# Gated linear attention in fp32: a gate product from three stacked exact parts, and scores from stacked keys

## The chip, the cores and the metric

The kernel runs on one core of one Trainium2 chip. The metric is the device time of one execution in microseconds (us), lower is better; 1022.12 us is the median of three runs before the change.

## What is computed

One decoder layer over 16 meta tokens and 256 real ones (272 positions, width 2048), all in float32. The mixing half of the layer has four heads of gated linear attention beside a pooling part; the MLP with a hidden width of 8192 follows. Cut to what the change touches:

```python
glr = u @ w_in[:, 3072:3088]                     # (272, 16), u = RMSNorm(h)
g_raw = glr @ gate_w2 + gate_b                   # (272, 512): 4 heads x 128
logg = log_sigmoid(g_raw) / 16
# per head and chunk of 64 tokens:
G = cumsum(logg)
q_dec = q * exp(G);  k_inv = k * exp(-G)
scores = where(causal, q_dec @ k_inv.T, 0)       # (64, 64)
o = scores @ v + q_dec @ S_prev                  # S_prev: state of all chunks before
```

The 256 real tokens are handled as two tiles of 128, that is as two pairs of chunks. Inside a tile the scores of the second chunk with keys of the first are also taken as scores, with their own decay, so that only one state per tile is needed.

## The kernel before, in words

Weights come in blocks of 128 x 2048 (1 MB) over the SP queue, always in the same order. To keep float32 accuracy with fast products, every operand is split into a rounded part `hi` (type fp32r, made by a ScalarE copy, L76) and the rest `lo` (VectorE subtraction, L77), and a product is made of three fp32r calls: hi x hi, hi x lo, lo x hi. Some small products are left as plain fp32 calls.

The stages in order: key projection while the input arrives (L238 to L259), the 16-wide gate projection (L303 to L315), four value strips, two query strips (`ws_strip`, L203 to L205), two strips for the output gate (`as_chunk`, L218 to L220), four pooling strips, the output projection, the first group of the MLP, and from about 300 us on seven repeats of a group stage (`group`, `product` L778 to L780, `half`) that holds most of the time. Small steps of the attention ride along in a list, `side`: after each half block of a strip one entry is taken (`run_side`). There `log_gates` (the gate product at L329, its vector work at L330 to L337), `gates` (L346: sums of the log gates by L353 and L363, exponentials, key products at L365 to L371), `states`, `scores` (L449) and `output` stand one after the other.

The order on each engine is not simply that of the program. The framework plans it from priorities, which follow the program's order, and from its own costs for every instruction, and adds the waits; each engine then works its list in order.

The gate projection makes `glrT`: 48 rows, of which 0 to 15 hold the product with the rounded weight columns, 32 to 47 the product with their rest, the others zero. The gate product (L329) multiplies it with `g2`, 48 rows that hold `gate_w2` twice at the same places, in fp32, once for the 16 meta tokens and once for each tile of 128. In `scores` each tile has two fp32 calls: `ki` (128 keys) with 128 queries, and `ke` (64 keys of the first chunk, decayed to its end) with the 64 queries of the second. Two masked copies (L461) and one ScalarE copy (L464) bring them to `sc`:

```python
pe.matmul(ps[:, ts], ki[h][:, ts], qd[h][:, ts], start=True, stop=True)          # L454
pe.matmul(ps[:64, 256 + 64 * t : 320 + 64 * t],                                  # L455
          ke[h][:, 144 + 64 * t : 208 + 64 * t], qd[h][:, t * P + 64 : (t + 1) * P], ...)
```

Of the kernel before, what the change touches and what calls it, by code (L numbers as in the profile page):

```python
# [7 lines left out]
F32 = mybir.dt.float32  # L8
F32R = mybir.dt.float32r
I32 = mybir.dt.int32  # L10
AF = mybir.ActivationFunctionType
ALU = mybir.AluOpType
PSUM = bass.MemoryType.PSUM

P = 128
D = 2048
KD = D // P
S = 256
NT = S // P
META = 16  # L20
L = META + S
H = 4
# [9 lines left out]
C_TRI, C_AFH, C_AFT, C_AFM, C_ID, C_ONE, C_MASK = 0, 128, 192, 320, 336, 464, 592  # L32
# [4 lines left out]
def hybrid_gla_pool_kernel(  # L37
# [15 lines left out]
    act, dve, pe = nc.scalar, nc.vector, nc.tensor  # L53
# [12 lines left out]
    gq = gstack.enter_context(tc.tile_pool(name="gq", bufs=1))  # L66

    def acc():
        return accp.tile([P, 512], F32, tag="acc", name="acc")

    def gp():
        return gpp.tile([P, 512], F32, tag="gp", name="gp")


    def split(raw, hi, lo):
        act.copy(out=hi, in_=raw)  # L76
        dve.tensor_tensor(out=lo, in0=raw, in1=hi.bitcast(F32), op=ALU.subtract)  # L77
# [40 lines left out]
    ps = gp()  # L118
# [6 lines left out]
    u_hi = big.tile([P, KD, L], F32R, tag="u_hi", name="u_hi")  # L125
    u_lo = big.tile([P, KD, L], F32R, tag="u_lo", name="u_lo")
# [13 lines left out]

    early = gq.tile([P, 768], F32, tag="gw0", name="early")
    glr_raw, gb = early[:, 512:], early[:, :512]
    g2 = gq.tile([48, 512], F32, tag="gw1", name="g2")
    gnw = gq.tile([P, DV], F32, name="gnw")


# [80 lines left out]
    for c in range(4):  # L227
# [6 lines left out]
        for o, n in steps:  # L234
            st = load_x(4 * c + o, n)
            for j in range(n):
                xs[o + j] = st[:, j]
            nc.sync.dma_start(  # L238
                out=raw[:, o * 512 : (o + n) * 512], in_=wts[c, :, o * 512 : (o + n) * 512]
            )  # L240
        w = []
        for hf in range(2):
            hi = hip.tile([P, 1024], F32R, tag="hi", name="hi")
            lo = lop.tile([P, 1024], F32R, tag="lo", name="lo")
            for j in (2 * hf, 2 * hf + 1):
                make_u(4 * c + j, xs[j])
                cs = slice((j % 2) * 512, (j % 2 + 1) * 512)
                split(raw[:, j * 512 : (j + 1) * 512], hi[:, cs], lo[:, cs])
            w.append((hi, lo))
        for jj in ((0,), (1,), (2, 3)) if c == 0 else ((0, 1), (2, 3)) if c < 3 else ((0, 1, 2, 3),):  # L250
            for m in range(H):
                for j in jj:
                    k = 4 * c + j
                    hi, lo = w[j // 2]
                    o = kp[m][:, :L]
                    cs = slice((j % 2) * 512 + m * P, (j % 2) * 512 + (m + 1) * P)
# [11 lines left out]
    kT = [gq.tile([P, L], F32, name=f"kT{h}") for h in range(H)]  # L268
# [27 lines left out]
    def ws_next(lo_t=0):  # L296
        nonlocal ci
        a, b = ci, ci + 1
        ci += 2
        return ws_strip([lambda: raw_chunk(a), lambda: raw_chunk(b)], lo_t)  # L300


    gl = gq.tile([P, KD, 48], F32R, tag="vn2", name="gl")  # L303
    glr_v = glr_raw.rearrange("p (k c) -> p k c", c=RANK)
    dve.memset(gl.bitcast(F32), 0.0)
    act.copy(out=gl[:, :, 0:16], in_=glr_v)
    dve.tensor_tensor(
        out=gl[:, :, 32:48], in0=glr_v, in1=gl[:, :, 0:16].bitcast(F32), op=ALU.subtract
    )
    ps = acc()  # L310
    for k in range(KD):
        pe.matmul(ps[:48, :L], gl[:, k, :], u_hi[:, k, :], start=k == 0, stop=False)
        pe.matmul(ps[:48, :L], gl[:, k, :], u_lo[:, k, :], start=False, stop=k == KD - 1)
    glrT = gq.tile([48, L], F32, name="glrT")
    act.copy(out=glrT, in_=ps[:48, :L])  # L315


    lgs = []
# [1 line left out]
    def log_gates():  # L320
        lg, l_hi, l_lo = (mp.tile([P, 3, 512], d, tag="m", name="lg") for d in (F32, F32R, F32R))
        lgs.extend((l_hi, l_lo))
        g = mp.tile([P, 3, 512], F32, tag="m", name="g")
        dve.memset(g[:, 2], 0.0)
        for t in (2, 0, 1):
            n = P if t < 2 else META
            o = META + t * P if t < 2 else 0
            ps = gp()
            pe.matmul(ps[:n], glrT[:, o : o + n], g2, start=True, stop=True)  # L329
            dve.scalar_tensor_tensor(  # L330
                out=g[:n, t], in0=ps[:n], scalar=rstd[:n, t : t + 1], in1=gb[:n], op0=ALU.mult, op1=ALU.add
            )
        act.activation(lg, g, AF.Abs)
        act.activation(lg, lg, AF.Exp, scale=-1.0)
        act.activation(lg, lg, AF.Ln, bias=1.0)
        dve.scalar_tensor_tensor(out=lg, in0=g, scalar=0.0, in1=lg, op0=ALU.min, op1=ALU.subtract)
        split(lg, l_hi, l_lo)  # L337

    eG = [gq.tile([P, S], F32, name=f"eG{h}") for h in range(H)]
    ki = [gq.tile([P, S], F32, name=f"ki{h}") for h in range(H)]  # L340
    ke = [gq.tile([P, L], F32, name=f"ke{h}") for h in range(H)]
    ken = [gq.tile([P, 2 * DK], F32, name=f"ken{h}") for h in range(H)]
    dtot = gq.tile([P, H], F32, name="dtot")

# [1 line left out]
    def gates(h, t):  # L346
        hs = slice(h * DK, (h + 1) * DK)
        ps = gp()
        if t < 2:
            n = 320 if t == 0 else 192  # L350
            r = cr[:, C_TRI : C_TRI + n]
            for i in range(2):
                pe.matmul(ps[:, :n], lgs[i][:, t, hs], r, start=i == 0, stop=i == 1)  # L353
            ts = slice(t * P, (t + 1) * P)
            act.activation(eG[h][:, ts], ps[:, 0:128], AF.Exp)
            act.activation(ki[h][:, ts], ps[:, 0:128], AF.Exp, scale=-1.0)
            act.activation(ke[h][:, 144 + 64 * t : 208 + 64 * t], ps[:, 128:192], AF.Exp)
            if t == 0:
                act.activation(ke[h][:, 16:144], ps[:, 192:320], AF.Exp)
        else:  # L360
            r = cr[:META, C_AFM : C_AFM + META]
            for i in range(2):
                pe.matmul(ps[:, :META], lgs[i][:META, 2, hs], r, start=i == 0, stop=i == 1)  # L363
            act.activation(ke[h][:, :META], ps[:, :META], AF.Exp)
            dve.tensor_tensor(out=ki[h], in0=kT[h][:, META:], in1=ki[h], op=ALU.mult)  # L365
            dve.tensor_tensor(out=ke[h][:, :144], in0=kT[h][:, :144], in1=ke[h][:, :144], op=ALU.mult)
            kv = ke[h][:, 144:].rearrange("p (t c) -> p t c", t=2)
            dve.tensor_tensor(
                out=kv, in0=kT[h][:, META:].rearrange("p (t c) -> p t c", t=2)[:, :, :64], in1=kv, op=ALU.mult
            )  # L370
            dve.tensor_tensor(  # L371
                out=dtot[:, h : h + 1], in0=eG[h][:, 63:64], in1=eG[h][:, 127:128], op=ALU.mult
            )

    def k_natural(h):
# [4 lines left out]
        act.copy(out=ken[h][:META, P : 2 * P], in_=ps[:META, P : 2 * P])  # L380

    side += [log_gates, idle, idle, idle, idle]
    for h in range(H):
        for t in range(2):
            side.append(lambda h=h, t=t: [gates(h, i) for i in ((0,), (1, 2))[t]])
# [29 lines left out]
    qd = [gq.tile([P, S], F32, name=f"qd{h}") for h in range(H)]  # L415
    qi = [gq.tile([P, S], F32, name=f"qi{h}") for h in range(H)]
    st = mp.tile([P, H, 2, DV], F32, tag="m", name="st")
    sc = [gq.tile([P, S], F32, name=f"sc{h}") for h in range(H)]
# [30 lines left out]
    def scores(h):  # L449
        ps = gp()  # L450
        dve.memset(sc[h], 0.0)
        for t in range(2):
            ts = slice(t * P, (t + 1) * P)
            pe.matmul(ps[:, ts], ki[h][:, ts], qd[h][:, ts], start=True, stop=True)  # L454
            pe.matmul(  # L455
                ps[:64, 256 + 64 * t : 320 + 64 * t], ke[h][:, 144 + 64 * t : 208 + 64 * t],
                qd[h][:, t * P + 64 : (t + 1) * P], start=True, stop=True,
            )
        for t in range(2):
            ts = slice(t * P, (t + 1) * P)  # L460
            dve.copy_predicated(  # L461
                out=sc[h][:, ts], mask=cst[:, C_MASK : C_MASK + P].bitcast(I32), data=ps[:, ts]
            )
        act.copy(  # L464
            out=sc[h][:64].rearrange("p (t c) -> p t c", t=2)[:, :, 64:],
            in_=ps[:64, 256:384].rearrange("p (t c) -> p t c", t=2),
        )

    def output(h, t):
        vs = slice(h * DV, (h + 1) * DV)  # L470
# [18 lines left out]
    for i in range(2):  # L489
        p = ws_next(META)  # L490
# [103 lines left out]
    for g in range(4):  # L594
        p = ws_next(META - (2 << g))
# [11 lines left out]
    h = lp.tile([P, NT, D], F32, name="h")  # L607
# [140 lines left out]
    for s in range(2):  # L748
        ps = [acc(), acc()]
# [3 lines left out]
        for t in range(NT):  # L753
            r = zt.tile([P, 512], F32, tag="r", name="r")
# [147 lines left out]
    for s in range(4):  # L902
# [13 lines left out]
        for t, strips in todo:  # L916
            for q in strips:
                parts = 2 if (t, q) == (1, 3) else 1
                w = 512 // parts
                for i in range(parts):  # L920
                    ps = acc()
                    for k in range(8):
                        hi, lo = tail[q][k // 2]
                        cs = slice((k % 2) * 512 + i * w, (k % 2) * 512 + (i + 1) * w)
                        ts = slice(t * P, (t + 1) * P)
# [4 lines left out]
                    if a + w == D:  # L930
# [4 lines left out]
                        out=h[:, t, a : a + w], in0=h[:, t, a : a + w], in1=fw[:, a : a + w], op=ALU.mult  # L935
# [39 lines left out]
def _constants(np):  # L975
    c = np.zeros((P, N_CONST), np.float32)
    i = np.arange(P)
    same = (i[:, None] // 64) == (i[None, :] // 64)
    upto = same & (i[:, None] <= i[None, :])
    c[:, C_ID : C_ID + P] = np.eye(P)  # L980
    c[:, C_TRI : C_TRI + P] = upto / 16.0
    c[:, C_AFH : C_AFH + 64] = (same & (i[:, None] > i[None, :]))[:, :64] / 16.0
    c[:, C_AFT : C_AFT + P] = (i[:, None] > i[None, :]) / 16.0
    c[:, C_ONE : C_ONE + P] = 1.0
    c[:, C_MASK : C_MASK + P] = upto
    j = np.arange(META)
    c[:META, C_AFM : C_AFM + META] = (j[:, None] > j[None, :]) / 16.0
    return c
# [40 lines left out]
```

## Time and profile before

| | |
|---|---|
| median of three runs | 1022.12 us (1021.54 to 1022.52) |
| the profiled execution's own time | 1019.51 us |
| its span, first to last instruction | 1017.7 us |
| TensorE matmul busy | 1001.1 us (98%) |
| TensorE weight loads busy | 843.9 us (83%) |
| VectorE busy | 829.4 us (81%) |
| ScalarE busy | 600.6 us (59%) |
| mean DMA rate | 194 GB/s |

PE is TensorE's matmul, PEld its weight load, DVE VectorE, ACT ScalarE, SP the queue that issues the loads. A line such as `L329 PE MATMUL gp<-g,glrT 48*16 48x512 x6` reads: program line, engine, operation, output tile from its inputs, rows and columns of the weights, shape of the streamed operand, number of records. Matmuls are pipelined, so records overlap and a record's length is not its cost; the step from one start to the next is. Where a record stands as started together with its own weight load, it waited for that load.

### The profile page before, as it was taken

The page shows a single profiled execution, that of the slowest core. Times are in us where ns is not written, and L with a number is a line of the kernel's source. Part 1 is how long each engine was busy: PE and PEld are TensorE (multiplying, and loading weights), DVE is VectorE, ACT ScalarE, POOL GpSimd, SP SyncE. Part 2 cuts the span into 40 slices and gives each one's busy share as a digit, 9 for nine tenths or more (in the row PEclk, how much of TensorE's full clock was granted, in tenths as well). Part 3 has the DMA queues.
Part 4 walks back from the last instruction along what each step waited for, and adds up shares of the span by engine and source line. Part 5 has one row for each costly group of instructions (what it writes and reads, how often), then busy time and mean ns, then how long its engine had stood idle before and what let it go on. Part 6 is the DMA issues. An engine that isn't in the chain of part 4 may idle for free.

```text
span 1017.7 us, 12947 instructions
## 1 busy us (share of the span) xinstructions
PE 1001.1 (98%) x5073; PEld 843.9 (83%) x5073; DVE 829.4 (81%) x924; ACT 600.6 (59%) x770; POOL 0.2 (0%) x4
## 2 busy tenths in 40 slices
PE   8999999999999899999999999999999999999996
PEld 7999978998888787888888888888888888888885
DVE  7455644776567989979989998997997999899784
ACT  7547544354555655666576576567657657656651
POOL 0000000000000000000000000000000000000000
PEclk9999999999999999999999999999999999999998
DMA  9763443446545283672483565367257357534642
GB/s 342 288 238 138 155 156 131 151 146 252 205 168 196 98 344 109 223 287 109 185 295 141 204 215 203 132 256 272 83 207 289 125 207 252 200 140 153 221 152 83
DMA packets 29821, 197.15 MB, mean 194 GB/s; under 512 B 3456, under 2 KB 3968, under 8 KB 6704
## 3 DMA queue, kind: packets, MB, share of 16 engines
q1 hardware_dynamic: 29760, 196.32, 52.8%
q8 instruction: 40, 0.66, 0.3%
q14 instruction: 21, 0.17, 0.0%
HBM read 194.21 MB, written 2.10 MB: 193 GB/s over the span
## 4 chain that ended last, share of the span: by engine, by line
PE 94%; DVE 4%; DMA 1%; issue 1%; ACT 1%; SPq 0%; ACTq 0%; DVEq 0%
PE acc L219 15%; PE acc L220 15%; PE acc L218 15%; PE sa L779 5%; PE sa L780 5%; PE sa L778 5%; PE acc L203 4%; PE acc L204 4%; PE acc L205 4%; PE sd L779 3%; PE sd L780 2%; PE sd L778 2%; PE gp L629 2%; PE acc L927 1%; PE acc L928 1%; PE acc L926 1%
## 5 line engine op out<-in xcount | busy, mean ns | idle before, releaser
L77 DVE TENSOR_TENSOR lo<-raw,hi 128x1024 fp32r<-128x1024 f32 (+1 forms) x300 | 351.9, 1194 | 115.5 <-ACT hi L76 109.4
L76 ACT CAST hi<-raw 128x1024 fp32r<-128x1024 f32 (+1 forms) x300 | 307.8, 1031 | 211.0 <-PE acc L220 98.5
L76 ACT CAST hi<-blk 128x1024 fp32r<-128x1024 f32 x140 | 147.2, 1054 | 114.6 <-PE acc L220 93.5
L77 DVE TENSOR_TENSOR lo<-blk,hi 128x1024 fp32r<-128x1024 f32 x140 | 166.8, 1221 | 14.4 <-ACT hi L76 12.5
L220 PE MATMUL acc<-hi,z_lo 128*128 128x512 f32 x448 | 175.6, 392 | 0.0
L219 PE MATMUL acc<-lo,z_hi 128*128 128x512 f32 x448 | 175.4, 392 | 0.1
L218 PE MATMUL acc<-hi,z_hi 128*128 128x512 f32 x448 | 174.8, 391 | 0.0
L219 PEld LDWEIGHTS acc<-lo,z_hi 128*128 128x128 f32 x448 | 84.1, 188 | 17.3 <-DVE lo L77 0.4
L218 PEld LDWEIGHTS acc<-hi,z_hi 128*128 128x128 f32 x448 | 84.1, 188 | 17.2
L220 PEld LDWEIGHTS acc<-hi,z_lo 128*128 128x128 f32 x448 | 84.2, 188 | 16.9
L784 DVE TENSOR_TENSOR blk<-blk,raw 128x2048 f32<-128x2048 f32 x42 | 96.0, 2287 | 0.2
L203 PE MATMUL acc<-u_hi,hi 128*128 128x272 f32 (+4 forms) x320 | 92.7, 290 | 0.0
L204 PE MATMUL acc<-u_lo,hi 128*128 128x272 f32 (+4 forms) x320 | 91.3, 286 | 0.0
L205 PE MATMUL acc<-u_hi,lo 128*128 128x272 f32 (+4 forms) x320 | 91.2, 285 | 0.0
L780 PE MATMUL sa<-hi,al 128*128 128x512 f32 x224 | 87.3, 390 | 0.0
L779 PE MATMUL sa<-lo,ah 128*128 128x512 f32 x224 | 87.2, 390 | 0.0
L778 PE MATMUL sa<-hi,ah 128*128 128x512 f32 x224 | 87.2, 389 | 0.0
L203 PEld LDWEIGHTS acc<-u_hi,hi 128*128 128x128 f32 x320 | 60.3, 189 | 1.0 <-issue 0.8
L204 PEld LDWEIGHTS acc<-u_lo,hi 128*128 128x128 f32 x320 | 60.2, 188 | 0.1
L205 PEld LDWEIGHTS acc<-u_hi,lo 128*128 128x128 f32 x320 | 60.1, 188 | 0.0
L621 DVE TENSOR_TENSOR h<-acc,h 128x512 f32<-128x512 f32 (+1 forms) x71 | 46.4, 681 | 4.5 <-PE acc L928 3.6
L779 PEld LDWEIGHTS sa<-lo,ah 128*128 128x128 f32 x224 | 42.0, 188 | 8.8
(236 smaller groups left out, 1549.7 us busy)
## 6 DMA issues: line engine op xcount, KB each, us to landing
raw<-in_wts SPq DMA_DIRECT2D x147, 1024.0 KB, 4.8
blk<-in_wts SPq DMA_DIRECT2D x28, 1024.0 KB, 4.8
xn<-in_x SPq DMA_DIRECT2D x2, 1024.0 KB, 11.3
h<-in_x SPq DMA_DIRECT2D x2, 1024.0 KB, 7.1
out<-h SPq DMA_DIRECT2D x8, 256.0 KB, 2.8
xTs<-in_xT SPq DMA_DIRECT2D x3, 546.0 KB, 9.6
pw<-in_pool_w SPq DMA_DIRECT2D x4, 256.0 KB, 6.0
fw<-in_rows SPq DMA_DIRECT2D x1, 1024.0 KB, 4.4
```

Of the source, the lines that this page charges most:

```text
L76: act.copy(out=hi, in_=raw)
L77: dve.tensor_tensor(out=lo, in0=raw, in1=hi.bitcast(F32), op=ALU.subtract)
L203: pe.matmul(o, hi[:, cs], u_hi[:, k, lo_t:L], start=k == 0, stop=False)
L204: pe.matmul(o, hi[:, cs], u_lo[:, k, lo_t:L], start=False, stop=False)
L205: pe.matmul(o, lo[:, cs], u_hi[:, k, lo_t:L], start=False, stop=k == KD - 1)
L218: pe.matmul(ps[t], a_hi[:, k, ts], hi[:, cs], start=st, stop=False)
L219: pe.matmul(ps[t], a_hi[:, k, ts], lo[:, cs], start=False, stop=False)
L220: pe.matmul(ps[t], a_lo[:, k, ts], hi[:, cs], start=False, stop=sp)
L778: pe.matmul(ps, a_hi[:, k], hi[:, cs], start=start and k == 0, stop=False, **kw)
L779: pe.matmul(ps, a_hi[:, k], lo[:, cs], start=False, stop=False, **kw)
L780: pe.matmul(ps, a_lo[:, k], hi[:, cs], start=False, stop=k == 7, **kw)
L784: dve.tensor_tensor(out=dst, in0=dst, in1=src, op=ALU.add)
```

## The change

The gate projection's weights become 96 columns, three times rounded part and rest side by side (16 + 16). `glrT` becomes fp32r: rows 0 to 63 are rounded on the copy, rows 64 to 95 get what the rounding left. The gate weights come in as six copies of `gate_w2` (96 x 512) and are rounded into `g2r`; rows 32 to 63 hold the rest of the rounding. The gate product is then one fp32r call per tile, with rounded x rounded, rounded x rest and rest x rounded summed in its contraction rows.

For the scores, three key blocks of 64 stand side by side per tile in `kk`: the first chunk's keys, the same keys decayed to the chunk's end, the second chunk's keys. Queries of the first chunk are multiplied with blocks 0 and 1 (128 keys), those of the second with blocks 1 and 2; the mask becomes the causal one of 128 x 128, and the ScalarE copy of the cross block goes.

```diff
-    g2 = gq.tile([48, 512], F32, tag="gw1", name="g2")
+    g2 = gq.tile([96, 512], F32, tag="gw1", name="g2")
+    g2r = gq.tile([96, 512], F32R, name="g2r")
...
-    gl = gq.tile([P, KD, 48], F32R, tag="vn2", name="gl")
+    gl = gq.tile([P, KD, 96], F32R, tag="vn2", name="gl")
     glr_v = glr_raw.rearrange("p (k c) -> p k c", c=RANK)
-    dve.memset(gl.bitcast(F32), 0.0)
-    act.copy(out=gl[:, :, 0:16], in_=glr_v)
-    dve.tensor_tensor(
-        out=gl[:, :, 32:48], in0=glr_v, in1=gl[:, :, 0:16].bitcast(F32), op=ALU.subtract
-    )
+    for r in range(0, 96, 32):
+        act.copy(out=gl[:, :, r : r + 16], in_=glr_v)
+        dve.tensor_tensor(
+            out=gl[:, :, r + 16 : r + 32], in0=glr_v, in1=gl[:, :, r : r + 16].bitcast(F32), op=ALU.subtract
+        )
+    act.copy(out=g2r, in_=g2)
+    dve.tensor_tensor(out=g2r[32:64], in0=g2[32:64], in1=g2r[32:64].bitcast(F32), op=ALU.subtract)
     ps = acc()
     for k in range(KD):
-        pe.matmul(ps[:48, :L], gl[:, k, :], u_hi[:, k, :], start=k == 0, stop=False)
-        pe.matmul(ps[:48, :L], gl[:, k, :], u_lo[:, k, :], start=False, stop=k == KD - 1)
-    glrT = gq.tile([48, L], F32, name="glrT")
-    act.copy(out=glrT, in_=ps[:48, :L])
+        pe.matmul(ps[:96, :L], gl[:, k, :], u_hi[:, k, :], start=k == 0, stop=False)
+        pe.matmul(ps[:96, :L], gl[:, k, :], u_lo[:, k, :], start=False, stop=k == KD - 1)
+    glrT = gq.tile([96, L], F32R, name="glrT")
+    act.copy(out=glrT, in_=ps[:96, :L])
+    dve.tensor_tensor(out=glrT[64:96], in0=ps[64:96, :L], in1=glrT[64:96].bitcast(F32), op=ALU.subtract)
...
-            pe.matmul(ps[:n], glrT[:, o : o + n], g2, start=True, stop=True)
+            pe.matmul(ps[:n], glrT[:, o : o + n], g2r, start=True, stop=True)
...
-    ki = [gq.tile([P, S], F32, name=f"ki{h}") for h in range(H)]
-    ke = [gq.tile([P, L], F32, name=f"ke{h}") for h in range(H)]
+
+    kk = [gq.tile([P, 2, 3, 64], F32, name=f"kk{h}") for h in range(H)]
+    ke = [gq.tile([P, 144], F32, name=f"ke{h}") for h in range(H)]
...
-            act.activation(ki[h][:, ts], ps[:, 0:128], AF.Exp, scale=-1.0)
-            act.activation(ke[h][:, 144 + 64 * t : 208 + 64 * t], ps[:, 128:192], AF.Exp)
+            act.activation(
+                kk[h][:, t, 0::2], ps[:, 0:128].rearrange("p (c b) -> p c b", c=2), AF.Exp, scale=-1.0
+            )
+            act.activation(kk[h][:, t, 1], ps[:, 128:192], AF.Exp)
...
-            dve.tensor_tensor(out=ki[h], in0=kT[h][:, META:], in1=ki[h], op=ALU.mult)
-            dve.tensor_tensor(out=ke[h][:, :144], in0=kT[h][:, :144], in1=ke[h][:, :144], op=ALU.mult)
-            kv = ke[h][:, 144:].rearrange("p (t c) -> p t c", t=2)
-            dve.tensor_tensor(
-                out=kv, in0=kT[h][:, META:].rearrange("p (t c) -> p t c", t=2)[:, :, :64], in1=kv, op=ALU.mult
-            )
+            kv = kT[h][:, META:].rearrange("p (t c b) -> p t c b", t=2, c=2)
+            dve.tensor_tensor(out=ke[h], in0=kT[h][:, :144], in1=ke[h], op=ALU.mult)
+            for c, k0 in ((0, 0), (1, 0), (2, 1)):
+                dve.tensor_tensor(out=kk[h][:, :, c], in0=kv[:, :, k0], in1=kk[h][:, :, c], op=ALU.mult)
...
+        kf = kk[h].rearrange("p t c b -> p t (c b)")
         for t in range(2):
-            ts = slice(t * P, (t + 1) * P)
-            pe.matmul(ps[:, ts], ki[h][:, ts], qd[h][:, ts], start=True, stop=True)
-            pe.matmul(
-                ps[:64, 256 + 64 * t : 320 + 64 * t], ke[h][:, 144 + 64 * t : 208 + 64 * t],
-                qd[h][:, t * P + 64 : (t + 1) * P], start=True, stop=True,
-            )
+            for c in range(2):
+                cs = slice(t * P + c * 64, t * P + (c + 1) * 64)
+                pe.matmul(ps[:, cs], kf[:, t, 64 * c : 64 * c + P], qd[h][:, cs], start=True, stop=True)
...
-        act.copy(
-            out=sc[h][:64].rearrange("p (t c) -> p t c", t=2)[:, :, 64:],
-            in_=ps[:64, 256:384].rearrange("p (t c) -> p t c", t=2),
-        )
...
-    c[:, C_MASK : C_MASK + P] = upto
+    c[:, C_MASK : C_MASK + P] = i[:, None] <= i[None, :]
...
-    g2 = np.zeros((48, 512), np.float32)
-    g2[0:16] = f["gate_w2"][0]
-    g2[32:48] = f["gate_w2"][0]
+    g2 = np.tile(f["gate_w2"][0], (6, 1))
```

## Rows read from the trace of the kernel before

**Rows 1.** The page's part 4, shares of the chain that ended last.
```profile
PE 94%; DVE 4%; DMA 1%; issue 1%; ACT 1%; SPq 0%; ACTq 0%; DVEq 0%
```
**Rows 2.** Timeline of TensorE, 74.9 to 78.6: start, length, line, shapes, records.
```profile
75.28 2.94 PE L329 MATMUL gp<-g,glrT 48*16 48x512 f32 x6
...
78.39 0.29 PE L204 MATMUL acc<-u_lo,hi 128*128 128x272 f32 x1
```
**Rows 3.** Timeline of the weight loads, same stretch.
```profile
76.77 0.19 PEld L329 LDWEIGHTS gp<-g,glrT 48*128 48x128 f32 x1 [0.24 <-issue]
77.20 0.19 PEld L329 LDWEIGHTS gp<-g,glrT 48*128 48x128 f32 x1 [0.24 <-issue]
```
**Rows 4.** One program line, L353: records, shortest, median and longest in ns.
```profile
L353 PE MATMUL gp<-cr,lg x16: 251/291/391, 93.7 to 116.9; 128*128 128x320 f32 x8, 128*128 128x192 f32 x8
```
**Rows 5.** Timeline of TensorE at the end of the gate projection.
```profile
35.76 0.29 PE L313 MATMUL acc<-u_lo,gl 128*48 128x272 f32 x1
35.88 0.29 PE L203 MATMUL acc<-u_hi,hi 128*128 128x272 f32 x1
```
**Rows 6.** Timeline of VectorE, 75 to 90; in brackets the idle time before, and its end.
```profile
76.35 0.74 DVE L330 SCALAR_TENSOR_TENSOR g<-gp,rstd,early 16x512 f32<-16x512 f32 x1 [1.04 <-PE gp L329]
77.40 1.61 DVE L330 SCALAR_TENSOR_TENSOR g<-gp,rstd,early 128x512 f32<-128x512 f32 x2 [0.31 <-PE gp L329]
...
87.95 1.22 DVE L77 TENSOR_TENSOR lo<-raw,hi 128x1024 fp32r<-128x1024 f32 x1
```
**Rows 7.** Timeline of ScalarE at 79.
```profile
79.04 1.49 ACT L333 ACTIVATE lg<-g 128x1536 f32<-128x1536 f32 x1 [2.88 <-DVE g L330]
```
**Rows 8.** Timeline of the weight loads at 90.3.
```profile
90.30 0.19 PEld L205 LDWEIGHTS acc<-u_hi,lo 128*128 128x128 f32 x1
```
**Rows 9.** Timeline of ScalarE, 22 to 28.
```profile
23.17 0.40 ACT L306 CAST gl<-early 128x256 fp32r<-128x256 f32 x1
27.53 0.39 ACT L273 COPY kT<-acc 128x272 f32<-128x272 f32 x1 [3.95 <-PE acc L259]
```
**Rows 10.** Timeline of VectorE, 23 to 30.
```profile
24.13 0.42 DVE L307 TENSOR_TENSOR gl<-early,gl 128x256 fp32r<-128x256 f32 x1
29.04 0.44 DVE L271 COPY kT<-acc 128x272 f32<-128x272 f32 x1 [4.50 <-PE acc L259]
```
**Rows 11.** DMA issues of the first 60 us: KB each, us from issue to landing.
```profile
g<-in_gate_w SPq DMA_DIRECT2D x1, 96.0 KB, 10.2
```
**Rows 12.** Windows: busy us (records) of PE, PEld, DVE, ACT, POOL; clock, DMA share, GB/s.
```profile
14.00:32.00 18.00, 18.00 (x146) 17.99 (x145) 12.12 (x23) 12.28 (x26) 0.00 (x0) 1.00 1.02 403
...
79.00:117.00 38.00, 38.00 (x312) 37.37 (x310) 22.43 (x38) 26.38 (x54) 0.00 (x0) 1.00 0.40 143
```
**Rows 13.** Timeline of TensorE at the first head's scores.
```profile
136.34 0.39 PE L454 MATMUL gp<-qd,ki 128*128 128x128 f32 x2
136.66 0.33 PE L455 MATMUL gp<-qd,ke 128*64 128x64 f32 x2
...
137.93 0.40 PE L219 MATMUL acc<-lo,u_hi 128*128 128x512 f32 x1
138.16 0.40 PE L220 MATMUL acc<-hi,u_lo 128*128 128x512 f32 x1
```
**Rows 14.** Timeline of the weight loads at the first head's scores.
```profile
136.12 0.42 PEld L454 LDWEIGHTS gp<-qd,ki 128*128 128x128 f32 x2
```
**Rows 15.** Timeline of TensorE at 48.4: an fp32 call of 128 x 128.
```profile
48.42 0.38 PE L187 MATMUL gp<-dg,cst 128*128 128x128 f32 x2
```
**Rows 16.** One program line, L368, in ns.
```profile
L368 DVE TENSOR_TENSOR ke<-kT,ke x4: 284/286/289, 99.9 to 119.1; 128x128 f32<-128x128 f32 x4
```
**Rows 17.** Timeline of VectorE, 1 to 4.
```profile
2.24 1.09 DVE L451 MEMSET sc<- 128x256 f32 x4
```
**Rows 18.** Waits of TensorE from 70 us on: total us, times, longest.
```profile
PE acc L219 <- DVE lo L77: 2.6, 1, 2.6
PE sd L779 <- DVE lo L77: 2.1, 1, 2.1
```

## Prediction

> **What bounds the kernel now.** I read the chain that ended last first: 94% of it is TensorE work [rows 1]. So a microsecond taken from TensorE counts, if TensorE does not stop for another engine later. Next I read the two places that the change touches, in the timelines of TensorE and of its weight loads, then what the neighbouring engines have to spare there.
>
> **The gate product, before.** Three fp32 calls, 48 rows deep, show as six matmul records [rows 2]: an fp32 call runs as two passes. One pass of 512 columns takes 0.43 us (weight load at 76.77 to weight load at 77.20, [rows 3]), a call 0.86. An fp32r call is one pass: the gate sums make two fp32r calls for each of four heads and two tiles, and have 16 records [rows 4]. 512 fp32r columns take 0.23 us, L219 to L220 [rows 13]. There are also pauses where the form of the array changes. The pass after 77.20 starts at 77.63 and ends at 78.06; but L203 streams only at 78.26, one step of 0.13 before the L204 of 78.39 [rows 2]. That is 0.20 us: about 0.1 until the weight load is let in, and 0.1 for the load, which is not hidden then. There are three such changes: into 48 rows by 16 columns (a short load, about 0.1), from there to 128 columns, and out.
>
> **The gate product, after.** Three fp32r calls of one pass: 3 x (0.86 - 0.23) = 1.9 us saved with all pauses kept, 2.4 if 96 rows cause none. No row shows a 96-row product. The nearest form shows no pause: after the last product of 128 rows by 48 columns L203 follows in 0.12 us [rows 5]. But a 16-column product stays among the three, and so I keep the two pauses around it: 2.1 us. The Trainium skill ("TensorEngine Tiling (Array Packing)", Key Properties) says that changing the tiling mode drains TensorE, and lists modes of 32, 64 and 128 rows. By it 96 rows are no mode of their own, and the gain would lie nearer 2.4.
>
> **What the earlier gates run into.** The vector work behind the product does not get shorter: three L330 steps, 0.74 for the first and 1.61 for the other two, end at 79.01 [rows 6], and ScalarE's Abs starts at 79.04 [rows 7]. In the new kernel the first result is there 0.43 + 0.2 earlier (one pass of 0.23 for two of 0.43), so L330 starts at 76.35 - 0.63 = 75.7 and, VectorE now being the longer part, ends at 75.7 + 0.74 + 1.61 = 78.05. This chain thus moves 1.0 us, not 2.1. Through ScalarE's queue it carries a split that TensorE needs for the first query strip: its low part is done at 87.95 + 1.22 = 89.17 [rows 6], and the load of its first use is at 90.30 [rows 8], 1.1 us to spare. With TensorE 2.1 and the chain 1.0 earlier nothing is left to spare; so 2.1 is about the cap. I book 2.0.
>
> **Ahead of the gate product** the high and low rows are made. gl takes three ScalarE copies and three subtractions, in place of one each and a memset, at 0.40 [rows 9] and 0.42 [rows 10]. The copy of the 96 x 512 weights and the subtraction on 32 of its rows have twice gl's 256 columns: at most 0.8 each. That is 1.6 us more on either engine, and both idle there: ScalarE 3.95 us behind L306 [rows 9], VectorE 4.50 behind L307 [rows 10]. I book nothing; without that cover the glr product would wait for gl. That product's weights grow from 48 to 96 columns; its step of 0.12 to 0.13 is that of L203 with 128 columns beside it [rows 5]: nothing. glrT's third part is one more subtraction of 0.4 on VectorE; nobody needs glrT before 75 us. The load of the gate weights doubles from 96 to 192 KB. It lands 10.2 us after its issue [rows 11]; at the 403 GB/s of that stretch [rows 12] 96 KB more put off what is queued behind it on SP by 0.24 us. Its reader is needed at 75 and, waiting in ScalarE's queue, has those 3.95 us; of the blocks behind it the first goes to products at 35.9 [rows 5], where ScalarE's split of it already began behind L273 at 27.5 [rows 9]. Nothing.
>
> **The scores, before.** One head takes from the first stream of L454 at 136.34 to the point where fp32r products run undisturbed again (L219 at 137.93 less one step of 0.23): 1.36 us [rows 13]. In it are four fp32 calls, eight passes, and at every call the form changes between 128 and 64 columns. Two passes of L454 from 136.34, 0.11 each, would be streamed by 136.57; L455 is let in only at 136.66 [rows 13]: the same pause as above.
>
> **The scores, after.** Again four calls and eight passes, all with 128 x 128 weights and 64 streamed columns: the form does not change. What is a pass worth that loads 128 columns and streams 64? No row has one. Two passes of L187, with 128 loaded and 128 streamed, start 0.11 apart (two records of 0.27 within 0.38, [rows 15]); so a load of 128 columns or a stream of 128 is 0.11, a stream of 64 is 0.05. Upper end: load and stream one behind the other, 0.16. Lower end: the load hidden altogether, 0.05. I take 0.11, the load as the longer part with the stream beside it: the second load of L454 starts at 136.35 (two of 0.19 within 0.42 from 136.12, [rows 14]), when its first pass starts to stream. So 8 x 0.11 = 0.88, saved 0.48 a head, four heads 1.9 us. The ends: 8 x 0.16 = 1.28 saves 0.3 in all, 8 x 0.05 = 0.4 saves 3.8.
>
> The removed ScalarE copy of the cross block is off the path, and the masked copies stay two a head. In the gates the key products become four VectorE multiplications a head in place of three, one more of 0.29 less what the halved one saves [rows 16]: at most 1.2 us over four heads, on an engine that works 22.4 of the 38 us there [rows 12]. Nothing booked; if it were not covered, the splits behind them would come later by that 0.29.
>
> **Sum.** -2.0 - 1.9 = -3.9 us. The profiled execution took 1019.51 us, its span 1017.7; it becomes 1015.6. The runs' median, 1022.12, is 2.6 above the profiled one; the same saving gives **1018.2**.
>
> **The rivals.** (a) *Given back by the order of the instructions.* The order on each engine is not the program's: sc's memset of line 451 runs at 2.24 us [rows 17]. A planner sets it, and shorter products can turn VectorE's and ScalarE's order later, where TensorE already stops twice for VectorE's low parts, 2.6 and 2.1 us [rows 18]. If one such stop doubles, about 2.4 of the 3.9 are gone: 1020.6. Against it: both stops lie behind VectorE work that TensorE's own results start, so all of it should move along. Chance 0.15.
>
> (b) *Loads do not overlap streams in the scores.* They save 0.3, the sum is -2.3: 1019.8. Against it are the loads of [rows 14]. Chance 0.05. The Trainium skill states such a rule ("TensorE: Matmul & The Clock Gate", The mechanism, in Part 3): a weight load overlaps matmuls in flight only in another row group. The trace disagrees, since the load at 136.35 uses all 128 rows beside a stream that does.
>
> (c) *The log-gate chain becomes the bound.* If the planner puts one more 1.0 us ahead of that split on ScalarE, the gate saves 1.0 only: 1019.2. For it: the spare time is used up. Against it: the planner sees the same chain. Chance 0.07.
>
> (d) *Slower.* From 300 us on, seven group stages repeat. If the new order makes the low part late in each as it is in the first (2.1 us, [rows 18]), six more stops cost 12.6: +8.7, 1030.8. It decides once 5.9 us are lost, with three groups of the six. That no later group shows such a stop now speaks against it. Chance 0.04.
>
> (e) *It does not do what it says.* If a 96-row fp32r product took two passes, the scores alone would be left, -1.9: 1020.2. The records of [rows 4] speak against it. Chance 0.02.
>
> The forecast has the other 0.67.
>
> **How the numbers follow.** About 0.2% (2.0 us) is what a measurement of this kernel can tell from no change. Faster by more than that: the forecast, (b), (c) and a small part of (a), 0.81. Within it: most of (a), and (e), 0.14. Slower: (d) and a little for what I do not see, 0.05. The range: below, no pauses and half of the way to the lower end of a pass, -2.4 - 2.9 = -5.3, and 0.5 for the scatter of the runs: 1016.3. Above, it takes in (a), (b), (c) and (e): 1020.8.
>
> **What would show it.** Right: three gate records instead of six, 0.23 us apart or with a pause, and L203 streaming at about 76.2 instead of 78.26; score passes 0.11 apart without pauses, fp32r products back 0.9 us after the first; everything past 165 us earlier by 3.9, and the stops of [rows 18] as long as now. Wrong: six gate records; passes 0.16 apart; TensorE waiting near 88 us for a low part; new stops behind VectorE after 300 us.

## The result, and the profile after

The changed kernel's runs have a median of 1015.7 us (1015.07 to 1018.02), those of the kernel before beside them 1021.83; the ratio is 0.9946, 95% interval 0.9935 to 0.9958. Two repetitions on other occasions gave 0.995 (0.9938 to 0.9962) and 0.9956 (0.9944 to 0.9969). So it is faster, by some 0.5% where 0.38% was forecast. The median lies 0.6 us below the stated range; by the ratio on the median of the prediction it is 1016.6, inside. The profiled execution took 1015.81 us with a span of 1014.0: 3.7 us less than the one before.

Where the 3.7 us come from is read by laying the two TensorE timelines side by side, the same product in each:

| product | before | after | difference |
|---|---|---|---|
| last of the gate projection | 35.76 | 36.32 | +0.56 |
| first of the gate sums | 93.75 | 91.82 | -1.93 |
| first of the states | 132.42 | 130.49 | -1.93 |
| first of the head outputs | 165.01 | 161.25 | -3.76 |
| first of the second norm (L674) | 332.09 | 328.36 | -3.73 |
| last of the kernel | 1008.78 | 1005.10 | -3.68 |

The gate stretch gave 2.49 us, the scores 1.83, and the start took back 0.56. Nothing is added or lost behind 165 us.

The timeline of TensorE around the gate product after the change (start, length, line, tiles, columns, shape, records; it answers to [rows 2]):

```profile
75.41 0.38 PE L409 MATMUL gp<-cst,vT 128*16 128x128 f32 x2
75.55 0.37 PE L206 MATMUL acc<-u_hi,lo 128*128 128x272 f32 x1
75.76 0.39 PE L334 MATMUL gp<-g2r,glrT 96*16 96x512 f32 x1
75.98 0.29 PE L204 MATMUL acc<-u_hi,hi 128*128 128x272 f32 x1
76.11 0.45 PE L334 MATMUL gp<-g2r,glrT 96*128 96x512 f32 x1
76.40 0.29 PE L205 MATMUL acc<-u_lo,hi 128*128 128x272 f32 x1
76.53 0.41 PE L334 MATMUL gp<-g2r,glrT 96*128 96x512 f32 x1
76.77 0.29 PE L206 MATMUL acc<-u_hi,lo 128*128 128x272 f32 x1
```

Three records, each 0.22 to 0.29 us before the next start, with strip products put between them by the planner, which the prediction did not foresee. No pause of 0.2 is left.

The first head's scores, TensorE and then the weight loads (they answer to [rows 13, 14]):

```profile
134.42 1.00 PE L462 MATMUL gp<-qd,kk 128*128 128x64 f32 x8
135.23 0.48 PE L219 MATMUL acc<-hi,u_hi 128*128 128x512 f32 x1
135.55 0.39 PE L220 MATMUL acc<-lo,u_hi 128*128 128x512 f32 x1
```

```profile
134.19 1.09 PEld L462 LDWEIGHTS gp<-qd,kk 128*128 128x128 f32 x8
```

Eight passes; from 134.42 to L220 less one step of 0.23, 135.32, are 0.90 us, where 0.88 was forecast and 1.36 stood before. The loads, of 0.19 each, start (1.09 - 0.19) / 7 = 0.13 apart on average with the first one early, 0.11 among the others.

The start is the one part of the difference that the change did not make. ScalarE's split of the third piece of weights (the second half of the first block) waits longer for its load, here in the kernel before and then in the one after:

```profile
9.10 1.14 ACT L76 CAST hi<-raw 128x512 fp32r<-128x512 f32 x2 [0.91 <-DMA raw<-in_wts]
```

```profile
9.64 1.14 ACT L76 CAST hi<-raw 128x512 fp32r<-128x512 f32 x2 [1.51 <-DMA raw<-in_wts]
```

The enlarged gate weights are issued only at 13.54 us, when this delay of 0.54 us is already there. In the other nine profiles with the changed gate the end of the gate projection stands between 0.5 us earlier and 1.2 later than before, in the two with the old gate 0.2 and 0.4 earlier; each time all but 0.3 us of the shift is there at this split. It is scatter of the first loads.

TensorE's waits after the change, from 70 us on (they answer to [rows 18]):

```profile
PE acc L220 <- DVE lo L77: 2.6, 1, 2.6
PE sd L779 <- DVE lo L77: 2.1, 1, 2.1
```

The two stops are as long as they were.

### The profile page after: what moved, and what is told of

It is laid out like the page before. It is cut to its first block, busy times and chain, and to the rows that moved or that the text cites. A ratio compares the mean times of both kernels' runs of the same rounds, so it can differ in the third digit from the quotient of the medians.

```text
span 1014.0 us, 12942 instructions
## 1 busy us (share of the span) xinstructions
PE 996.7 (98%) x5070; PEld 843.2 (83%) x5070; DVE 830.3 (82%) x931; ACT 600.0 (59%) x769; POOL 0.2 (0%) x4
## 4 chain that ended last, share of the span: by engine, by line
PE 94%; DVE 4%; DMA 1%; ACT 1%; issue 1%; SPq 0%; ACTq 0%
PE acc L220 15%; PE acc L221 15%; PE acc L219 15%; PE sa L779 5%; PE sa L780 5%; PE sa L778 5%; PE acc L204 4%; PE acc L205 4%; PE acc L206 4%; PE sd L779 3%; PE sd L780 3%; PE sd L778 3%; PE gp L629 2%; PE acc L927 1%; PE acc L928 1%; PE acc L926 1%
## 5 line engine op out<-in xcount | busy, mean ns | idle before, releaser
L220 PE MATMUL acc<-lo,z_hi 128*128 128x512 f32 x448 | 175.4, 392 | 0.0
L220 PEld LDWEIGHTS acc<-lo,z_hi 128*128 128x128 f32 x448 | 84.1, 188 | 17.3 <-DVE lo L77 0.3
```

The costliest lines, as they stand in the source:

```text
L220: pe.matmul(ps[t], a_hi[:, k, ts], lo[:, cs], start=False, stop=False)
```

## The experiments

Theory A: the gain is what TensorE is spared at the two places, 4.3 us, and the rest of the measured difference is scatter. Theory B: the change gives something besides.

**The kernel again, and its two halves.** The first of these is the changed kernel unaltered; the other two take one part of its diff each.

> The changed kernel as it is, beside its two halves. Theory A (the gain is the work taken from TensorE at the two places, and all of it reaches the end): 2.5 us from the gate product and 1.85 from the scores, 4.3 in all, 0.9958 of before; the 5.5 us of the first comparison is then partly scatter between runs. Theory B (something besides, at the start or in a later order, gives about 1.5 us more): 0.9946 again.

```diff
 # gate part only: g2, g2r, gl, glrT and the host's g2 as changed
-            pe.matmul(ps[:n], glrT[:, o : o + n], g2, start=True, stop=True)
+            pe.matmul(ps[:n], glrT[:, o : o + n], g2r, start=True, stop=True)
```

> The gate part alone, scores as before. Theory A: the stretch around the gate product is 2.5 us shorter, everything behind it moves along, 0.9976 of before. Theory B: over 3.5 us, the surplus lies in the gate part (its loads, its gl and g2r steps, or the order). If ScalarE's chain behind the gates were the bound, as the prediction priced it, 2.0 us.

```diff
 # scores part only: kk, ke, the causal mask, scores() as changed
-            pe.matmul(ps[:, ts], ki[h][:, ts], qd[h][:, ts], start=True, stop=True)
+                pe.matmul(ps[:, cs], kf[:, t, 64 * c : 64 * c + P], qd[h][:, cs], start=True, stop=True)
```

> The scores part alone, gate product as before. Theory A: each head's scores 0.46 us shorter, 1.85 us in all, 0.9982 of before. Theory B: over 3 us, the surplus lies here.

Ratios: 0.995 for the whole, 0.9962 (0.995 to 0.9975) for the gate part, 0.9982 (0.9974 to 0.9991) for the scores. The ratios alone do not decide: that of the whole allows both theories, and that of the gate part, 3.9 us, lies on the side of theory B, with 0.9976 just outside its interval. The traces do. In them the gate part alone moves the gate sums by -2.48 us against its start, the scores alone each head by -0.46, 1.85 in all. So the halves add up to the 4.3 us, and neither holds a surplus. But the profile of the gate part ends 0.3 us later than that of before: it loses its gain at two places. TensorE's clock shows where (windows: busy us and records of PE, PEld, DVE, ACT, POOL, then the granted clock, DMA share, GB/s). First the gate part alone behind its two stops, then the changed kernel's first profile around its own two stops:

```profile
353.30:356.60 3.30, 3.30 (x9) 2.56 (x8) 3.30 (x4) 0.11 (x1) 0.00 (x0) 0.50 0.94 318
387.40:390.70 3.30, 3.30 (x9) 2.52 (x9) 3.30 (x4) 1.69 (x2) 0.00 (x0) 0.50 0.00 0
```

```profile
348.00:352.00 4.00, 1.42 (x8) 1.03 (x7) 4.00 (x5) 2.49 (x4) 0.00 (x0) 1.00 0.00 0
381.80:385.20 3.40, 1.30 (x6) 0.74 (x5) 3.40 (x3) 1.96 (x2) 0.00 (x0) 1.00 0.00 0
```

The same kernel can show either. Behind the first stop, the changed kernel in its first profile and in its second:

```profile
351.30:354.60 3.30, 3.30 (x15) 2.69 (x16) 3.30 (x5) 0.71 (x1) 0.00 (x0) 1.00 0.71 233
```

```profile
351.30:354.60 3.30, 3.09 (x7) 2.48 (x8) 3.30 (x5) 0.00 (x0) 0.00 (x0) 0.50 0.63 184
```

Behind each of the two stops, in some executions and not in others, the clock stands at 1.2 GHz instead of 2.4 for a stretch, and in the gate part's profile the products there come 1.6 and 1.4 us later. Of the 13 profiles of this study three show no such stretch, four one behind the first stop (in one of them that stop had moved), three one behind the second, three both. From 8 us to the last products none shows one anywhere else. The lists of runs tell the same by their mean clock. At 0.997 the kernel before has 5 runs of 33, median 1019.74; the changed one 7 of 16, median 1015.6: 4.1 us. At 0.994 before has 10, median 1022.67, the changed one 3, median 1018.02: 4.65. At equal clock, then, the difference is near the 4.3 us of theory A. The gate part alone gives 2.7 us that way (two runs at 0.997, median 1017.0). The 5.5 of the first medians fits more low-clock runs on the side of before: five of the changed kernel's six runs there stand at 0.997 (the six of before have no clock on record). Why there are more is open; with so few runs it may be chance.

**The third repetition.**

> The changed kernel a third time, same chip. Theory A (4.3 us from the two places, the rest of the measured difference is scatter from the clock behind the two stops and from the arrival of the first loads): ratio 0.9946 to 0.997, and at equal clock (0.997 with 0.997) 4.3 us less than before within 0.7.

0.9956 (0.9944 to 0.9969). Its one run at 0.997 took 1015.78 us, 4.0 less than the 1019.74 of before. Its profile ends the gate projection 0.8 us late and shows one stretch at half clock behind the first stop.

**What the pauses are worth in the scores.** This kernel and the two that follow (32 queries, 48 rows) ran once each, so only their traces are read. The old calls in another order:

```diff
             pe.matmul(ps[:, ts], ki[h][:, ts], qd[h][:, ts], start=True, stop=True)
+        for t in range(2):
             pe.matmul(
                 ps[:64, 256 + 64 * t : 320 + 64 * t], ke[h][:, 144 + 64 * t : 208 + 64 * t],
...
```

> The kernel before, with the score calls of a head in another order: both L454 first, then both L455, so that the form of the array changes twice a head and not four times. Theory A (the pauses at changes of form are a large part of what the change saves): a head's block goes from 1.36 to about 1.0 us, 1.4 us over four heads, though the same eight passes run. Rival (the saving comes from streaming fewer columns): 1.36 as before.

Its TensorE timeline at the first head:

```profile
135.85 0.61 PE L454 MATMUL gp<-qd,ki 128*128 128x128 f32 x4
136.39 0.45 PE L456 MATMUL gp<-qd,ke 128*64 128x64 f32 x4
136.77 0.50 PE L218 MATMUL acc<-hi,u_hi 128*128 128x512 f32 x1
137.10 0.39 PE L219 MATMUL acc<-lo,u_hi 128*128 128x512 f32 x1
```

From 135.85 to 137.10 - 0.23 are 1.02 us, 0.34 less than before. Of the 0.46 that the change saves a head, three quarters can be had by the order of the calls alone.

**What sets a pass.** Half of the streamed queries:

```diff
+                cs = slice(cs.start, cs.start + 32)
                 pe.matmul(ps[:, cs], kf[:, t, 64 * c : 64 * c + P], qd[h][:, cs], start=True, stop=True)
...
```

> The changed kernel with 32 streamed queries per score call instead of 64; half of the scores are left out. Theory A (a pass is as long as its load of 128 columns): still 0.11 us a pass, a head's block 0.9 us. Rival (stream and load in part behind each other): 0.03 us less a pass, block 0.65 to 0.7.

The second head of that kernel:

```profile
141.04 0.98 PE L463 MATMUL gp<-qd,kk 128*128 128x32 f32 x8
141.86 0.47 PE L219 MATMUL acc<-hi,u_hi 128*128 128x512 f32 x1
142.17 0.40 PE L220 MATMUL acc<-lo,u_hi 128*128 128x512 f32 x1
```

141.04 to 141.94: 0.90 us, as with 64 queries. A fixed price of a pass, whatever it loads, would show the same; the kernel with reordered calls speaks against it. Its loads of 64 columns:

```profile
136.39 0.31 PEld L456 LDWEIGHTS gp<-qd,ke 128*64 128x64 f32 x4
```

One of them takes 0.14 us, so four within 0.31 start 0.06 apart: half the columns, half the step. So the load of 128 columns sets the pass, 0.11 us, and the stream is hidden beside it.

**What 96 rows are worth.** The gate product over 48 of them:

```diff
-            pe.matmul(ps[:n], glrT[:, o : o + n], g2r, start=True, stop=True)
+            pe.matmul(ps[:n], glrT[:48, o : o + n], g2r[:48], start=True, stop=True)
```

> The changed kernel with the gate product over the first 48 of its 96 rows; the other rows' terms are left out. Theory A (48 rows are another form of the array than 128, 96 rows are not): pauses with open weight loads of about 0.2 us come back at each change, 0.4 to 1.2 us in all by how many products of other lines stand between. Rival (the pauses belonged to fp32): no difference beyond 0.05 us.

```profile
75.40 0.40 PE L334 MATMUL gp<-g2r,glrT 48*16 48x512 f32 x1
75.73 0.39 PE L204 MATMUL acc<-u_hi,hi 128*128 128x272 f32 x1
76.06 0.49 PE L334 MATMUL gp<-g2r,glrT 48*128 48x512 f32 x1
76.48 0.39 PE L205 MATMUL acc<-u_lo,hi 128*128 128x272 f32 x1
```

From one line's start to the next it now takes 0.33 to 0.42 us, where it was 0.13 to 0.29 with 96 rows; the gate stretch gains 1.49 us in place of 2.48. So in this order, with strip products between the calls and thus six changes, one of the 2.5 us comes from the depth and not from fp32r. Back to back, as the calls stood before, there would be three changes and less to gain from the depth; that was not run.

**The same for the other shallow products.** On top of the change, the products with 16 rows get 128, the added ones zeros. The transposes that feed the states become 128 columns wide too, and two ScalarE copies behind them become one:

```diff
-                pe.matmul(ps[:, :META], lgs[i][:META, 2, hs], r, start=i == 0, stop=i == 1)
+                pe.matmul(ps[:, :META], lgs[i][:, 2, hs], r, start=i == 0, stop=i == 1)
...
-    pe.matmul(ps[:, :DV], ken[h][:META, P : 2 * P], vn[2][:, vs], start=True, stop=True)
+    pe.matmul(ps[:, :DV], ken[h][:, P : 2 * P], vn[2][:, vs], start=True, stop=True)
```

> The changed kernel, and the other products with 16 rows made 128 rows deep by zeros (the sums of the meta tokens' gates, the first states, the spread of the meta tokens' norm). Theory A, by which a change in the array's rows costs a pause and an open weight load and the depth itself nothing: four times 0.3 us at the gate sums, four times 0.4 at the states, 0.3 at the norm, 3.1 us less than the changed kernel. Rival (the steps behind 16-row products are slow for another reason, such as waits for their inputs): no difference beyond 0.5 us.

> The kernel with all products 128 rows deep, again, to stand beside the spread one on the same chip. Both theories: 0.992 of before, the stops of 2.6 and 2.1 as they were; half clock behind one or both in part of the runs.

0.9918 (0.9905 to 0.9932) and 0.9939 (0.9925 to 0.9953), the second above the 0.992 expected for it. Beside the changed kernel's runs of the same occasions the medians are 3.2 and 2.5 us lower, where 3.1 was expected. In both traces TensorE at 260 us, counted from the end of the gate projection, is 2.8 us ahead of the changed kernel. First the changed kernel at the first head's states, then this one:

```profile
130.49 0.69 PE L446 MATMUL gp<-vn,ken 16*128 16x256 f32 x2
131.12 0.70 PE L449 MATMUL gp<-vn,ken 128*128 128x256 f32 x2
...
131.88 0.39 PE L220 MATMUL acc<-lo,u_hi 128*128 128x512 f32 x1
```

```profile
129.10 0.59 PE L446 MATMUL gp<-vn,ken 128*128 128x256 f32 x2
129.53 0.59 PE L449 MATMUL gp<-vn,ken 128*128 128x256 f32 x2
...
130.20 0.39 PE L220 MATMUL acc<-lo,u_hi 128*128 128x512 f32 x1
```

From the first stream to L220: 1.39 us with 16 rows, 1.10 with 128. A wait ahead of the first, about 0.1, is gone as well.

**The stops.** Two attempts at the one at 352 us, both on the kernel with full rows. The first moves four VectorE steps away:

```diff
-        dve.tensor_tensor(out=blk(*dst), in0=blk(*x0), in1=blk(*x1), op=op)
+        nc.gpsimd.tensor_tensor(out=blk(*dst), in0=blk(*x0), in1=blk(*x1), op=op)
```

> The kernel with all products 128 rows deep, and the four additions and subtractions of L705 on GpSimd instead of VectorE. Theory A (TensorE's stop at 352 us is VectorE's overload by the operands' preparation, and the stop lets the clock fall in some runs): VectorE has 4.9 us less between 347 and 365, the stop of 2.6 shrinks below 1, 1.5 to 2.5 us less than with the additions on VectorE, and no half clock at 352 in any profile; the stop at 386 stays. Rival (GpSimd's slower steps hold up the operands): the stop moves behind GpSimd and the time does not fall.

The rival held: 0.9957 (0.9943 to 0.9972), worse than without. GpSimd's timeline, then TensorE's waits:

```profile
340.88 13.44 POOL L705 TENSOR_TENSOR a<-a 128x1024 f32<-128x1024 f32 x4 [340.44 <-DVE al L696]
```

```profile
PE gp L629 <- DVE q L757: 4.3, 1, 4.3
PE sd L779 <- DVE lo L77: 2.1, 1, 2.1
PE acc L220 <- DVE lo L77: 0.6, 1, 0.6
```

A step of 1.22 us on VectorE takes 3.4 on GpSimd, and VectorE's own steps beside it (L696) take 2.4 and 2.8 in place of 1.2. ScalarE waits 4.2 us for the first GpSimd result, and VectorE behind it; the old stop shrinks to 0.6, and a longer one stands before L629. Behind that one the clock falls again in this profile, at 351 us, so what theory A says of the clock was not tested. The second attempt changes only how many steps one half block takes:

```diff
-            lambda: operand(2, 0, 1), s5, s7, s6, s3,
+            lambda: operand(2, 0, 1), *s5, *s7, s6, s3,   # s5 and s7 as lists of single steps
```

> The kernel with all products 128 rows deep, and the preparation of operands 5 and 7 split into single steps, so that one half block takes one of them and not two or three. The same work. Theory A (the stop at 352 us is a crowd of preparation steps in front of a low part, and the clock falls only in executions where TensorE has stopped): the stop of 2.6 shrinks below 1, 2 to 3 us less than with the crowd; profiles show no half clock near 352, and the runs scatter less. Rival (VectorE is behind by its whole work there, not by its order): the stop moves to a later half and the time is the same within 0.5 us.

0.9899 (0.9884 to 0.9914), median 1010.12 beside 1013.83 of the crowded one and 1020.9 of before: 3.7 us less than with the crowd, more than the 2 to 3 expected. Its waits of TensorE:

```profile
PE sd L780 <- DVE lo L77: 2.1, 1, 2.1
PE sd L779 <- ACT x L789: 0.2, 1, 0.2
```

The stop of 2.6 is gone, and the trace gains 3.0 us at that place; the rest of the 3.7 fits a clock that falls less often. Its four runs have clocks of 0.995 to 0.997, those of the crowded one 0.994 and 0.995; its profile has no half clock. That the runs scatter less is not shown: they lie 2.5 us apart, the crowded ones 3.2. This is the fastest version of the study.

## Why the prediction was right, and where it was not

**The chain.** Right: TensorE bounds the kernel, and what it was spared reached the end. The traces differ by -3.76 us at 165 and by -3.68 at the end.

**The scores.** Right in mechanism and size: 0.90 us a head for a forecast of 0.88, 1.85 in all for 1.9. That the load sets the pass is shown by the kernel with 32 queries and the shorter loads of the one with reordered calls, that form changes were the greater part by the latter. Rival (b), loads not beside streams, falls with both. The rule that the Trainium skill gives ("TensorE: Matmul & The Clock Gate", The mechanism), overlap only in another row group, does not describe this trace: these loads use all 128 rows beside streams that do. The same section also names a load into a background weight buffer; the prediction left that case out.

**The gate product.** Mis-sized, 2.5 us for a booked 2.0, by two steps. First, "I keep the two pauses around it": with 96 rows none was left, even with 16 columns. The Trainium skill's rule on modes ("TensorEngine Tiling (Array Packing)", Key Properties) pointed the right way, and the kernel with 48 rows, at 1.0 us less gain, agrees with it for rows. Second, the cap "nothing is left to spare" rested on a wrong pairing: the low part done at 89.17 [rows 6] is not the one whose first use is loaded at 90.30 [rows 8]. In the changed kernel the same first use is at 88.55, where VectorE has done only the first of these two:

```profile
86.37 2.35 DVE L77 TENSOR_TENSOR lo<-raw,hi 128x1024 fp32r<-128x1024 f32 x2
```

```profile
88.55 0.19 PEld L206 LDWEIGHTS acc<-u_hi,lo 128*128 128x128 f32 x1
```

The two are done at about 87.6 and 88.7. Which one the load reads is found by counting: it opens the seventeenth half block of the strips, and the first of the two is the seventeenth split of such a half block. In the kernel before the seventeenth is this one:

```profile
81.72 1.23 DVE L77 TENSOR_TENSOR lo<-raw,hi 128x1024 fp32r<-128x1024 f32 x1 [2.71 <-ACT hi L76]
```

It was done seven us ahead of its use, so there was no cap at 2.1. The chain did move less than TensorE, as forecast: ScalarE's Abs starts at 78.27 where it was 79.04 [rows 7], 1.3 us earlier against the late start.

**The covers** held: gl's six steps, g2r and the doubled load end before 26.6, and TensorE has no gap at the gate projection.

**The order of the instructions** (rivals (a) and (c)) did change: the split that ran at 80.64 runs at 84.92. It cost nothing here, but it took most of what was to spare: of the seven us one is left in the changed kernel. No new stop appeared (rival (d)), and each call is one pass (rival (e) fell).

**The run-to-run part** was missing. I set 0.5 us for the scatter; the stops of [rows 18] let the clock fall in some executions at about 1.5 us each, so that runs of one kernel lie 4 us apart. This put the median below the range; the 0.4 us that the forecast lacked would not have.

## What to carry to other kernels

Look at what stands between small products before their own length: a product of 16 or 48 rows among products of 128 costs its pauses and weight loads that no stream hides, and rows of zeros, or stacked parts that fill the rows, take them away. With few streamed columns the load of the stationary side sets the pace, so calls of one form in a row are worth more than fewer columns. Before a trace's wait is made a cap, find by counting which buffer the waiting instruction reads.

## What the runs showed of the hardware

A stop of TensorE of 2.1 to 2.6 us was followed, in some executions only, by a stretch at 1.2 GHz, worth about 1.5 us; two such places explain most of the scatter of this kernel's times: before the change, the runs at a mean clock of 0.994 and of 0.997 have medians 2.9 us apart, and all runs lie within 4 us. A product of 96 rows by 16 columns in fp32r cost no more than 0.1 us beside its stream, while 48 rows, 16 rows, and in fp32 128 rows by 64 columns each brought pauses. In fp32r 128 rows by 48 columns brought none [rows 5]; 64 columns in fp32r were not tried.
